# Moving a matmul's two operands apart in SBUF, and alternating the columns of the moving one

## The chip, the cores and the metric

The kernel runs on one core of a Trainium2 chip. The metric is the device time of one execution in microseconds (us). Before the change three runs took 2104.46, 2105.78 and 2109.65 us; the median, 2105.78 us, is what the change is held against.

## The reference

Two layers work on 256 tokens of width 2048, all in fp32. The first mixes by a wide causal convolution and a pooling branch, the second by a short gated convolution; each is followed by a gated feed-forward part of width 5632.

```python
h = x
for i in range(DEPTH):                       # DEPTH = 2
    j = i // 2
    if i % 2 == 0:
        h = h + conv_pool_mixer(h, mix_norm_e[j], w_in_e[j], conv_w_e[j], ...)
    else:
        h = h + short_conv_mixer(h, mix_norm_o[j], w_in_o[j], conv_w_o[j], w_out_o[j])
    h = h + swiglu(rms_norm(h, ffn_norm[i]), w_gate[i], w_up[i], w_down[i])
return rms_norm(h, final_norm)

def swiglu(h, w_gate, w_up, w_down):
    return (jax.nn.silu(h @ w_gate) * (h @ w_up)) @ w_down
```

Everything that is costly in it is a product of 256 tokens with a weight matrix. All weights together are some 5,900 blocks of 128x128.

## The kernel before, in words

Activations lie transposed: features on the 128 partitions, the 256 tokens (`T`) along the free dimension, a tensor of 2048 features as 16 chunks. Each weight block is used once. Blocks stream from HBM in the order of their use (`fetch`, L100, up to 16 blocks of 64 KB to a DMA on SP's queue), and `prepare` (L106) splits eight of them at a time into two float32r tiles: `hi`, a rounded copy made by ScalarE (L114), and `lo`, the rest, made by VectorE (L121, by GpSimd for a range of blocks in the first mixer). Activations are split in the same way by `split` (L193): a chunk of a moving tensor is 512 columns, first the 256 of its high half and then the 256 of its low half, 2048 bytes in each partition.

`product` (L161) multiplies one block with one chunk. In the wide form (all of both feed-forward parts but their last output chunk, and the whole second mixer) it issues two matmuls: `hi` with all 512 columns (L163, the high halves' product lands in the left half of a PSUM bank and the cross term in the right), and `lo` with the 256 high columns, added to the right half (L164). In the narrow form (the first mixer, and the last output chunk) there are three matmuls of 256 columns (L166 to L168). Every matmul comes with a weight load of its own (LDWEIGHTS, PEld in the profile), which reads 128 columns of `hi` or `lo`, 512 bytes in each partition, while the matmul before it streams.

The stages, in order of time: the first mixer (narrow; its moving tensors are `xs`, the normalized input, and `cat`, the mixer's inner result); then the first feed-forward part in two halves, each of 704 wide products on `xs` and 352 on `y` (the gated inner result); the second mixer with 768 wide products on `xs` and 256 on `z`; and the second feed-forward part like the first, with 330 wide and 22 narrow products on the last `y`. The order of the work on each engine comes from a scheduler when the program is built. It is the same, instruction by instruction, before and after the change on all five engines; only operands' addresses and patterns differ.

Where the operands lie matters for what follows. In the built program each `hi` and `lo` tile starts at 64 modulo 256 bytes, and blocks in it are 512 bytes apart, so every weight load starts at 64 modulo 256. `xs` starts at 64, `cat` at 96, `y` and `z` at 160 modulo 256, and their chunks are 2048 bytes apart. Each moving operand therefore stands at one fixed distance past its weights, modulo 256: `xs` at 0, `cat` at 32, `y` and `z` at 96 bytes. (The low half of a chunk starts 1024 bytes behind the high half, which is the same place modulo 256.)

Of the kernel before, what the change touches and what calls it, by code (L numbers as in the profile page):

```python
# [12 lines left out]
F32R = mybir.dt.float32r  # L13
# [4 lines left out]
P = 128  # L18
T = 256
D = 2048  # L20
NC = D // P
DC = 1024
NA = DC // P
FF = 5632
NF = FF // P
NH = NF // 2
# [40 lines left out]
PIECE = 8  # L67
PIECES = [(u, o, min(PIECE, n - o)) for u, n in enumerate(UNITS) for o in range(0, n, PIECE)]

LOOK = 4  # L70
AHEAD = 1

WARM = 9

KEEP = 8

POOL_SPLIT = range(96, 24 * NC + 16 + 7 * NC + 8)

# [6 lines left out]
def block_kernel(ctx: ExitStack, tc: tile.TileContext, xT: bass.AP, xtok: bass.AP, vec: bass.AP, wall: bass.AP, out: bass.AP):  # L85
    nc = tc.nc
    const = ctx.enter_context(tc.tile_pool(name="const", bufs=1))
    act = ctx.enter_context(tc.tile_pool(name="act", bufs=1))
# [8 lines left out]
    cursor = [0, 0]  # L97
    relief = []

    def fetch(u):  # L100
        if u < len(UNITS) and u not in loaded:
            n, off = UNITS[u], UNIT_AT[u] * P * P
            loaded[u] = w = wst.tile([P, 16 * P], F32, name="w")
            nc.sync.dma_start(w[:, : n * P], wall[off : off + n * P * P].rearrange("(p f) -> p f", p=P))  # L104

    def prepare(i):  # L106
        if i >= len(PIECES) or i in ready:
            return
        u, o, n = PIECES[i]
        fetch(u)  # L110
        w = loaded[u][:, o * P : (o + n) * P]
        hi = whl.tile([P, PIECE * P], F32R, name="hi")
        lo = whl.tile([P, PIECE * P], F32R, name="lo")
        nc.scalar.copy(hi[:, : n * P], w)  # L114
        engine = nc.vector
        if UNIT_AT[u] + o in POOL_SPLIT:
            if relief:
                relief.pop()
            else:
                engine = nc.gpsimd  # L120
        engine.tensor_tensor(out=lo[:, : n * P], in0=w, in1=hi[:, : n * P], op=ALU.subtract)  # L121
        ready[i] = (hi, lo)

    def next_block():
        b, i = cursor
        at = UNIT_AT[PIECES[i][0]] + PIECES[i][1]
# [28 lines left out]
    def drain():  # L155
        while any(queues.values()):
            for q in queues.values():
                if q:
                    q.popleft()[1]()

    def product(acc, hi, lo, x, first, last, wide):  # L161
        if wide:
            nc.tensor.matmul(acc, hi, x, start=first, stop=False, skip_group_check=True)  # L163
            nc.tensor.matmul(acc[:, T:], lo, x[:, :T], start=False, stop=last, skip_group_check=True)  # L164
        else:
            nc.tensor.matmul(acc[:, :T], hi, x[:, :T], start=first, stop=False)  # L166
            nc.tensor.matmul(acc[:, :T], hi, x[:, T:], start=False, stop=False)  # L167
            nc.tensor.matmul(acc[:, :T], lo, x[:, :T], start=False, stop=last)  # L168

    def matmul_chunks(xs, ks, n=1, wide=False, behind=None):  # L170


        accs = [ps.tile([P, 2 * T], F32, name="acc") for _ in range(n)]
        for i, k in enumerate(ks):
            first, last = i == 0, i == len(ks) - 1
            for acc in accs:
                hi, lo = next_block()
                product(acc, hi, lo, xs[:, k, :], first, last, wide)
                tick()
            if behind is not None:  # L180
                behind(k)
        return accs
# [22 lines left out]
    def col(name, i):  # L205
        return v[:, VECS[name] + i : VECS[name] + i + 1]

    identity = v[:, VECS["identity"] :]
    h = act.tile([P, NC, T], F32, name="h")
    xs = act.tile([P, NC, 2 * T], F32R, name="xs")  # L210
    ones = const.tile([P, P], F32, name="ones")
    nc.gpsimd.memset(ones, 1.0)

# [14 lines left out]
    def rsqrt_of(*totals, scale, halves=False, st=None):  # L228
# [42 lines left out]
    class Norm:  # L271


        def __init__(self, gain, final=False):
            self.gain, self.final = gain, final
            self.sums = []

        def add(self, c):
# [6 lines left out]

        def scale(self, c):
            if not self.final:
                split(xs[:, c, :], h[:, c, :], col(self.gain, c))

        def square(self, c):  # L290
            if c == 0:
# [37 lines left out]
        return s  # L329


    norm = Norm("mix_norm_e")
    nc.sync.dma_start(v[:, :NC], vec[:, :NC])

    def load(at, n):
# [30 lines left out]
    every = range(NC)  # L366
    with tc.tile_pool(name="m0", bufs=1) as m0, tc.tile_pool(name="ps_side", bufs=2, space=PSUM) as ps_side:
# [1 line left out]
        a_in = m0.tile([P, NA, pad + T], F32, name="a_in")  # L369
        nc.gpsimd.memset(a_in[:, :, :pad], 0.0)  # L370
        conv = m0.tile([P, NA, T], F32, name="conv")
        cat = m0.tile([P, NA, 2 * T], F32R, name="cat")
        total = m0.tile([P, 2, T], F32, name="total")

        sides, prods, state = {}, {}, {}
# [113 lines left out]
        first = matmul_chunks(xs, every, n=4, behind=loads_behind)  # L489
# [42 lines left out]

        project(xs, POOL_CHUNKS)
        drain()
        norm = Norm("ffn_norm0")
        project(cat, range(NA), norm)

    def swiglu(norm, following):
        with tc.tile_pool(name="ffn", bufs=1) as fp:
            phase[0] = fp  # L540
            y = fp.tile([P, NH, 2 * T], F32R, name="y")
            r = None
            for half in range(2):
                for f in range(NH):
                    (acc_g,) = matmul_chunks(xs, every, wide=True)
                    (acc_u,) = matmul_chunks(xs, every, wide=True)
                    if r is None:
                        r = norm.rstd()
                    gate = scaled(acc_g, r, "gate", True)
                    up = scaled(acc_u, r, "val", True)  # L550
                    nc.scalar.activation(gate, gate, AF.Silu)
                    nc.vector.tensor_tensor(out=up, in0=up, in1=gate, op=ALU.mult)
                    split(y[:, f, :], up)
                project(y, range(NH), following if half else None, wide=True, narrow_end=half and following.final)
# [1 line left out]
    x0.close()  # L556


    after = Norm("mix_norm_o")
    swiglu(norm, after)  # L560


    norm = Norm("ffn_norm1")
    with tc.tile_pool(name="m1", bufs=1) as m1:
        phase[0] = m1
        z = m1.tile([P, NC, 2 * T], F32R, name="z")
        pad = SW - 1
        r = None
        for c in range(NC):
            (acc_c,) = matmul_chunks(xs, every, wide=True)  # L570
            (acc_v,) = matmul_chunks(xs, every, wide=True)
# [12 lines left out]
            (acc_b,) = matmul_chunks(xs, every, wide=True)  # L584
# [7 lines left out]
    swiglu(norm, last)  # L592
# [93 lines left out]
```

## Time and profile before

| what | value |
|---|---|
| median of three runs | 2105.78 us |
| the profiled execution, its own time | 2103.73 us |
| its span in the profile | 2102.0 us |
| TensorE (PE) busy | 2079.1 us, 99% |
| weight loads (PEld) busy | 1855.8 us, 88% |
| VectorE (DVE), ScalarE (ACT), GpSimd (POOL) busy | 66%, 50%, 10% |
| HBM traffic | 187 GB/s over the span |

The profiled execution lies 2 us below the median and 1.7 us above its span, so a saving read from the trace can be taken off the median as it stands. Busy time of PE is no measure of how well it works: a matmul's end is modelled, and one is shown as running while the next has begun. What can be trusted are the starts, and so the distance from one start to the next; I call it the pitch.

### The profile page before, as it was taken

The page shows a single profiled execution, that of the slowest core. Times are in us where ns is not written, and L with a number is a line of the kernel's source. Part 1 is how long each engine was busy: PE and PEld are TensorE (multiplying, and loading weights), DVE is VectorE, ACT ScalarE, POOL GpSimd, SP SyncE. Part 2 cuts the span into 40 slices and gives each one's busy share as a digit, 9 for nine tenths or more (in the row PEclk, how much of TensorE's full clock was granted, in tenths as well). Part 3 has the DMA queues.
Part 4 walks back from the last instruction along what each step waited for, and adds up shares of the span by engine and source line. Part 5 has one row for each costly group of instructions (what it writes and reads, how often), then busy time and mean ns, then how long its engine had stood idle before and what let it go on. Part 6 is the DMA issues. An engine that isn't in the chain of part 4 may idle for free.

```text
span 2102.0 us, 31608 instructions
## 1 busy us (share of the span) xinstructions
PE 2079.1 (99%) x12584; PEld 1855.8 (88%) x12584; DVE 1383.4 (66%) x1979; ACT 1060.9 (50%) x1571; POOL 200.6 (10%) x180
## 2 busy tenths in 40 slices
PE   8999999999999999999999999999999999999998
PEld 8999988888888888888888888888888888888887
DVE  6888866666556666666777777666666556666654
ACT  7776654444444444454444445554444444444453
POOL 3985200000000000011000001100000000000011
PEclk9999999999999999999999999999999999999999
DMA  8554455555555555555555555555555555555551
GB/s 326 187 191 168 158 184 197 183 198 182 194 185 188 193 187 194 183 196 182 183 198 182 198 183 193 180 189 198 183 196 184 189 192 183 198 182 199 182 192 68
DMA packets 56884, 395.53 MB, mean 188 GB/s; under 512 B 6432, under 2 KB 7200, under 8 KB 9760
## 3 DMA queue, kind: packets, MB, share of 16 engines
q1 hardware_dynamic: 56736, 393.52, 52.4%
q8 instruction: 98, 1.61, 0.3%
q14 instruction: 50, 0.41, 0.1%
HBM read 391.39 MB, written 2.10 MB: 187 GB/s over the span
## 4 chain that ended last, share of the span: by engine, by line
PE 98%; DMA 1%; DVE 1%; ACT 0%; SPq 0%; issue 0%; DVEq 0%; ACTq 0%
PE acc L163 57%; PE acc L164 30%; PE acc L166 4%; PE acc L168 4%; PE acc L167 4%; DMA rows<-in_xtok 0%; DMA h<-in_xT 0%; DVE res L603 0%; ACT hi L114 0%; PE st L237 0%; PE st L268 0%; DVE lo L121 0%; SPq L104 0%; ACT conv L475 0%; PE idle L243 0%
## 5 line engine op out<-in xcount | busy, mean ns | idle before, releaser
L114 ACT CAST hi<-w 128x1024 fp32r<-128x1024 f32 (+1 forms) x740 | 776.1, 1050 | 975.3 <-PE acc L163 621.0
L121 DVE TENSOR_TENSOR lo<-w,hi 128x1024 fp32r<-128x1024 f32 (+1 forms) x691 | 845.2, 1224 | 639.5 <-ACT hi L114 635.3
L163 PE MATMUL acc<-xs,hi 128*128 128x512 f32 x3584 | 1243.3, 391 | 0.0
L164 PE MATMUL acc<-xs,lo 128*128 128x256 f32 x3584 | 1004.7, 280 | 0.0
L163 PEld LDWEIGHTS acc<-xs,hi 128*128 128x128 f32 x3584 | 670.4, 187 | 146.2
L164 PEld LDWEIGHTS acc<-xs,lo 128*128 128x128 f32 x3584 | 678.1, 189 | 0.1
L163 PE MATMUL acc<-y,hi 128*128 128x512 f32 x1386 | 485.2, 393 | 0.0
L164 PE MATMUL acc<-y,lo 128*128 128x256 f32 x1386 | 386.4, 279 | 0.0
L163 PEld LDWEIGHTS acc<-y,hi 128*128 128x128 f32 x1386 | 259.4, 187 | 61.7
L164 PEld LDWEIGHTS acc<-y,lo 128*128 128x128 f32 x1386 | 259.9, 187 | 0.4
L298 POOL TENSOR_TENSOR sumsq<-sumsq,sq 128x256 f32<-128x256 f32 x56 | 58.8, 1050 | 1599.1 <-ACT sq L296 1599.1
L166 PE MATMUL acc<-xs,hi 128*128 128x256 f32 x512 | 144.0, 284 | 5.2 <-ACT hi L114 4.2
L167 PE MATMUL acc<-xs,hi 128*128 128x256 f32 x512 | 143.6, 283 | 0.0
L168 PE MATMUL acc<-xs,lo 128*128 128x256 f32 x512 | 141.3, 284 | 0.1
L121 POOL TENSOR_TENSOR lo<-w,hi 128x1024 fp32r<-128x1024 f32 x49 | 118.7, 2441 | 43.1 <-PE acc L167 34.3
L166 PEld LDWEIGHTS acc<-xs,hi 128*128 128x128 f32 x512 | 98.1, 192 | 6.2 <-ACT hi L114 5.0
L167 PEld LDWEIGHTS acc<-xs,hi 128*128 128x128 f32 x512 | 98.2, 192 | 0.0
L168 PEld LDWEIGHTS acc<-xs,lo 128*128 128x128 f32 x512 | 96.5, 192 | 0.5 <-DVE lo L121 0.5
L163 PE MATMUL acc<-z,hi 128*128 128x512 f32 x256 | 89.6, 393 | 0.0
L188 ACT COPY cross<-acc 128x256 f32<-128x256 f32 x224 | 80.6, 360 | 0.0
L164 PE MATMUL acc<-z,lo 128*128 128x256 f32 x256 | 71.3, 279 | 0.0
L318 DVE TENSOR_TENSOR h<-acc,h 128x256 f32<-128x256 f32 x112 | 47.2, 423 | 18.9 <-PE acc L168 13.2
(134 smaller groups left out, 1198.6 us busy)
## 6 DMA issues: line engine op xcount, KB each, us to landing
w<-in_wall SPq DMA_DIRECT2D x365, 1024.0 KB, 4.8
w<-in_wall SPq DMA_DIRECT2D x7, 512.0 KB, 7.7
rows<-in_xtok SPq DMA_DIRECT2D x2, 1024.0 KB, 7.9
h<-in_xT SPq DMA_DIRECT2D x7, 256.0 KB, 7.3
out<-res SPq DMA_DIRECT2D x2, 512.0 KB, 2.8
out<-res SPq DMA_DIRECT2D x2, 384.0 KB, 2.8
v<-in_vec SPq DMA_DIRECT2D x1, 260.0 KB, 6.7
h<-in_xT SPq DMA_DIRECT2D x2, 128.0 KB, 2.3
```

Of the source, the lines that this page charges most:

```text
L114: nc.scalar.copy(hi[:, : n * P], w)
L121: engine.tensor_tensor(out=lo[:, : n * P], in0=w, in1=hi[:, : n * P], op=ALU.subtract)
L163: nc.tensor.matmul(acc, hi, x, start=first, stop=False, skip_group_check=True)
L164: nc.tensor.matmul(acc[:, T:], lo, x[:, :T], start=False, stop=last, skip_group_check=True)
L166: nc.tensor.matmul(acc[:, :T], hi, x[:, :T], start=first, stop=False)
L167: nc.tensor.matmul(acc[:, :T], hi, x[:, T:], start=False, stop=False)
L168: nc.tensor.matmul(acc[:, :T], lo, x[:, :T], start=False, stop=last)
L188: nc.scalar.copy(t, acc[:, T:])
L298: nc.gpsimd.tensor_tensor(out=self.sums[0], in0=self.sums[0], in1=sq, op=ALU.add)
L318: nc.vector.tensor_tensor(out=h[:, n, :], in0=acc[:, :T], in1=h[:, n, :], op=ALU.add)
```

## The change

Two things about the moving operand of a matmul change. No instruction is added, removed or moved to another place in any engine's order.

First, where it lies. The moving tensors get tiles with some room at the end, and a helper places them at a chosen byte offset in that room. In the built program `xs` now stands 32 bytes past its weights modulo 256 in the first mixer and 160 past them afterwards, `cat` 32 (as before), and `y` and `z` 160.

Second, in the wide form the order in which the columns of the first matmul (on `hi`) are streamed. Where it was the 256 high columns and then the 256 low ones, it may now be `w` high ones, `w` low ones, the next `w` high ones, and so on. The output is addressed by the same pattern, so every column still lands where it did. `w` depends on the stage: columns in the old order (`w` = 0) in the first half of the first feed-forward part, 32 in its second half, 64 in the second mixer, 8 in the first half of the second feed-forward part and 16 in its second half. The second matmul (on `lo`), and the narrow form, keep their order.

```diff
+_m0, _ffn = 24 * NC + 16 + NC * NC, 3 * NH * NC
+ORDER = {_m0: 0, _m0 + _ffn: 32, _m0 + 2 * _ffn: 64, _m0 + 2 * _ffn + 64 * NC: 8, _m0 + 3 * _ffn + 64 * NC: 16}
...
+XS_M0 = 32
+XS_F0 = 160
+XS_M1 = 160
+XS_F1 = 160
+Y_F0 = 64
+Y_F1 = 64
+Z_M1 = 64
+CAT = 0
...
     def product(acc, hi, lo, x, first, last, wide):
         if wide:
-            nc.tensor.matmul(acc, hi, x, start=first, stop=False, skip_group_check=True)
+            w = ORDER[max(b for b in ORDER if b < cursor[0])]
+            out, x2 = (a.rearrange("p (h b w) -> p b h w", h=2, w=w) if w else a for a in (acc, x))
+            nc.tensor.matmul(out, hi, x2, start=first, stop=False, skip_group_check=True)
             nc.tensor.matmul(acc[:, T:], lo, x[:, :T], start=False, stop=last, skip_group_check=True)
...
-    xs = act.tile([P, NC, 2 * T], F32R, name="xs")
+    xs_room = act.tile([P, NC * 2 * T + 64], F32R, name="xs")
+
+    def moving(room, at, n):
+
+        return room[:, at // 4 : at // 4 + n * 2 * T].rearrange("p (c t) -> p c t", c=n)
...
     class Norm:
-        def __init__(self, gain, final=False):
+        def __init__(self, gain, at=0, final=False):
             self.gain, self.final = gain, final
+            self.xs = moving(xs_room, at, NC)
...
         def scale(self, c):
             if not self.final:
-                split(xs[:, c, :], h[:, c, :], col(self.gain, c))
+                split(self.xs[:, c, :], h[:, c, :], col(self.gain, c))
...
-        cat = m0.tile([P, NA, 2 * T], F32R, name="cat")
+        cat = moving(m0.tile([P, NA * 2 * T + 32], F32R, name="cat"), CAT, NA)
...
-            y = fp.tile([P, NH, 2 * T], F32R, name="y")
+            y = moving(fp.tile([P, NH * 2 * T + 32], F32R, name="y"), at, NH)
...
-        z = m1.tile([P, NC, 2 * T], F32R, name="z")
+        z = moving(m1.tile([P, NC * 2 * T + 32], F32R, name="z"), Z_M1, NC)
```

More of the change, by code (lines that the diff above doesn't have):

```diff
@@ L329, in scaled @@
         return s
-    norm = Norm("mix_norm_e")
+    norm = Norm("mix_norm_e", XS_M0)
+    xs = norm.xs
     nc.sync.dma_start(v[:, :NC], vec[:, :NC])
@@ L534, in block_kernel, with swiglu @@
         drain()
-        norm = Norm("ffn_norm0")
+        norm = Norm("ffn_norm0", XS_F0)
         project(cat, range(NA), norm)
-    def swiglu(norm, following):
+    def swiglu(norm, following, at):
         with tc.tile_pool(name="ffn", bufs=1) as fp:
             phase[0] = fp
-            y = fp.tile([P, NH, 2 * T], F32R, name="y")
+            y = moving(fp.tile([P, NH * 2 * T + 32], F32R, name="y"), at, NH)
             r = None
@@ L544, in swiglu @@
                 for f in range(NH):
-                    (acc_g,) = matmul_chunks(xs, every, wide=True)
-                    (acc_u,) = matmul_chunks(xs, every, wide=True)
+                    (acc_g,) = matmul_chunks(norm.xs, every, wide=True)
+                    (acc_u,) = matmul_chunks(norm.xs, every, wide=True)
                     if r is None:
@@ L556, in block_kernel @@
     x0.close()
-    after = Norm("mix_norm_o")
-    swiglu(norm, after)
-    norm = Norm("ffn_norm1")
+    after = Norm("mix_norm_o", XS_M1)
+    swiglu(norm, after, Y_F0)
+    norm = Norm("ffn_norm1", XS_F1)
     with tc.tile_pool(name="m1", bufs=1) as m1:
         phase[0] = m1
-        z = m1.tile([P, NC, 2 * T], F32R, name="z")
+        z = moving(m1.tile([P, NC * 2 * T + 32], F32R, name="z"), Z_M1, NC)
         pad = SW - 1
@@ L569, in block_kernel @@
         for c in range(NC):
-            (acc_c,) = matmul_chunks(xs, every, wide=True)
-            (acc_v,) = matmul_chunks(xs, every, wide=True)
+            (acc_c,) = matmul_chunks(after.xs, every, wide=True)
+            (acc_v,) = matmul_chunks(after.xs, every, wide=True)
             if r is None:
@@ L583, in block_kernel @@
                 nc.vector.scalar_tensor_tensor(out=co, in0=cv[:, k : k + T], scalar=v[:, wc + k : wc + k + 1], in1=co, op0=ALU.mult, op1=ALU.add)
-            (acc_b,) = matmul_chunks(xs, every, wide=True)
+            (acc_b,) = matmul_chunks(after.xs, every, wide=True)
             bg = scaled(acc_b, r, "pv", True)
@@ L591, in block_kernel @@
     last = Norm("final_norm", final=True)
-    swiglu(norm, last)
+    swiglu(norm, last, Y_F1)
     halves = rsqrt_of(*last.sums, scale=1.0 / D, halves=True)
```

## The prediction

> **What bounds the kernel now.** I read the engines' shares first, then the groups, and then the busy time by stage, with the stages' bounds set where the moving tensor changes.
>
> ```profile
> span 2102.0 us, 31608 instructions
> PE 2079.1 (99%) x12584; PEld 1855.8 (88%) x12584; DVE 1383.4 (66%) x1979; ACT 1060.9 (50%) x1571; POOL 200.6 (10%) x180
> PE 98%; DMA 1%; DVE 1%; ACT 0%; SPq 0%; issue 0%; DVEq 0%; ACTq 0%
> ...
> L163 PE MATMUL acc<-xs,hi 128*128 128x512 f32 x3584 | 1243.3, 391 | 0.0
> L164 PE MATMUL acc<-xs,lo 128*128 128x256 f32 x3584 | 1004.7, 280 | 0.0
> L163 PE MATMUL acc<-y,hi 128*128 128x512 f32 x1386 | 485.2, 393 | 0.0
> L163 PE MATMUL acc<-z,hi 128*128 128x512 f32 x256 | 89.6, 393 | 0.0
> L166 PE MATMUL acc<-xs,hi 128*128 128x256 f32 x512 | 144.0, 284 | 5.2 <-ACT hi L114 4.2
> ```
>
> 98% of the chain that ended last is PE, and the wide matmuls (L163, L164) have no idle time before them. So nothing feeds PE too late; the only question is how long each matmul occupies it. The mean of 391 ns is no answer, since matmuls overlap in these records. The pitch is read from the stages. The rows below are, in this order, the stages on `xs`, `y`, `xs`, `y`, `xs`, `z`, `xs`, `y`, `xs`, `y`; columns are the stretch, its length, each engine's busy time and instructions, the granted clock, and the DMA engines' share and GB/s.
>
> ```profile
> 259.47:504.89 245.42, 245.42 (x1421) 216.60 (x1420) 159.22 (x228) 120.94 (x179) 0.19 (x1) 1.00 0.53 189
> 504.89:628.13 123.24, 123.24 (x706) 107.54 (x705) 67.06 (x78) 51.59 (x61) 0.00 (x0) 1.00 0.52 188
> 628.13:872.19 244.06, 244.06 (x1410) 215.33 (x1409) 157.29 (x218) 117.69 (x175) 0.00 (x0) 1.00 0.54 190
> 872.19:995.43 123.24, 123.24 (x706) 107.54 (x705) 79.72 (x93) 62.40 (x91) 13.93 (x14) 1.00 0.53 188
> 995.43:1263.03 267.60, 267.60 (x1548) 236.15 (x1547) 192.87 (x295) 120.60 (x163) 1.52 (x16) 1.00 0.53 189
> 1263.03:1352.67 89.64, 89.64 (x514) 78.09 (x513) 65.13 (x83) 49.00 (x79) 13.83 (x14) 1.00 0.53 188
> 1352.67:1598.08 245.41, 245.41 (x1420) 216.58 (x1419) 159.54 (x229) 119.80 (x179) 0.19 (x1) 1.00 0.53 189
> 1598.08:1721.33 123.25, 123.25 (x707) 107.41 (x705) 67.14 (x78) 51.62 (x61) 0.00 (x0) 1.00 0.53 188
> 1721.33:1965.39 244.06, 244.06 (x1410) 215.35 (x1409) 157.28 (x218) 117.65 (x175) 0.00 (x0) 1.00 0.54 190
> 1965.39:2080.92 115.53, 115.53 (x662) 100.64 (x661) 60.13 (x71) 57.82 (x83) 17.52 (x13) 1.00 0.42 150
> sum 1821.45, PE 1821.45 PEld 1601.23 DVE 1165.39 ACT 869.12 POOL 47.18; mean PE 182.15 PEld 160.12 DVE 116.54 ACT 86.91 POOL 4.72
> ```
>
> These stages hold 1821.45 of the 2102.0 us, at a full granted clock (1.00), with PE never idle, while DVE is busy 73% at most (65.13 of 89.64) and the DMA engines 54%. One wide product, a pair of matmuls with 512 and 256 columns, takes 244.06 / 704 = 346.7 ns on `xs` and 123.24 / 352 = 350.1 ns on `y`; on `z` it is 89.64 / 256 = 350.2. Same instructions, same columns, same engine loads; `xs` lies 0 and `y` and `z` 96 bytes past the weights modulo 256. That is a first sign that the distance matters, if a small one: 1%.
>
> The narrow form gives a second. The first row is a stretch wholly on `xs` (distance 0), the second wholly on `cat` (distance 32), both of 256-column matmuls; after it four starts in a row on `cat`, and two on `xs`.
>
> ```profile
> 60.00:140.00 80.00, 80.00 (x669) 80.00 (x668) 71.90 (x133) 62.76 (x113) 73.56 (x42) 1.00 0.53 187
> 222.00:258.00 36.00, 36.00 (x311) 36.00 (x310) 33.04 (x43) 24.88 (x43) 11.61 (x13) 1.00 0.51 179
> ```
>
> ```profile
> 239.76 0.28 PE L168 MATMUL acc<-cat,lo 128*128 128x256 f32 x1
> 239.87 0.28 PE L166 MATMUL acc<-cat,hi 128*128 128x256 f32 x1
> 239.99 0.28 PE L167 MATMUL acc<-cat,hi 128*128 128x256 f32 x1
> 240.11 0.28 PE L168 MATMUL acc<-cat,lo 128*128 128x256 f32 x1
> 240.23 0.28 PE L166 MATMUL acc<-cat,hi 128*128 128x256 f32 x1
> ...
> 100.16 0.28 PE L167 MATMUL acc<-xs,hi 128*128 128x256 f32 x1
> 100.28 0.28 PE L168 MATMUL acc<-xs,lo 128*128 128x256 f32 x1
> ```
>
> The counts hold the two or three matmuls that overlap a stretch's edge (0.28 us shown each, at a pitch of 0.12). Without them 80.00 / 666.7 = 120.0 ns on `xs`, 36.00 / 308.7 = 116.6 on `cat`: 3.4 ns, or 2.8%, for 32 bytes of distance. On `cat` the pitch is uneven, one in four about 0.11 us and the others 0.12, so a matmul there can go faster than any on `xs`. DVE and ACT don't make the difference: PE had no idle time in either stretch.
>
> My reading: while a matmul streams its moving columns, the next weight load reads 512 bytes of the same partitions; where both want the same part of memory, the stream stops for a moment, and the distance decides how often.
>
> **The first part: the distance.** In the first mixer `xs` goes from 0 to 32, where `cat` has been all along. 512 narrow products of three matmuls at 3.4 ns make 5.2 us. The idle time of 5.2 us before L166 is no part of the pitch, and DVE's 71.90 of 80.00 us leaves room for 3%. Between nothing (where this stage waits for weights anyway) and 5.2 I take 4.5 us.
>
> For the wide form the distance of 160 is nowhere in this trace. The bounds come from the nearest rows. On the bad side a pair costs what it costs at 96: 350.1 ns, so the 3584 pairs on `xs` lose 3.4 ns each, 12 us, and the 1642 on `y` and `z` stay. On the good side every matmul comes down as far as the fastest one in four on `cat`, an estimate of 113.3 ns (four pitches make 466 at a mean of 116.6; with three of them near 118 some 113 are left), 6.7 ns below `xs`: 13.4 per pair on `xs`, to 333.3, and 16.8 on `y` and `z`: 48 + 28 = 76 us. Between them lies `cat`'s mean: 3.4 ns for a matmul, 6.8 a pair, so 340 ns, from 346.7 and 350.1. I take this one, because it is the only other distance whose effect is measured per weight load, and the load is the same in both forms. 3584 x 6.7 = 24.0 and 1642 x 10.1 = 16.6: **40.6 us**.
>
> The page "TensorE: Matmul & The Clock Gate" of the Trainium skill (Step-by-step: what each phase is for) has it otherwise: the array has two independent read ports, and loading the next weights takes no read bandwidth from the running matmul. By that rule the distance is worth nothing and the 40.6 us are 0. The 120.0 against 116.6 ns here do not agree with it.
>
> **The second part: the order of columns.** It touches only the `hi` matmul, on 1056 pairs with `w` = 32, 1024 with 64, 1056 with 8 and 1034 with 16; 1056 keep the old order. No row of this trace has a matmul with such a pattern. It moves no byte more. What it changes is how fast the moving address advances: two blocks of `w` columns start at the same place modulo 256, so with 8, 16 and 32 the position advances half as fast on average, while with 64 columns (256 bytes) it goes round as before. If the weight load advances more slowly than the stream, which the trace does not resolve, the two might keep their distance and meet less. The best that can be is again 333.3 ns a pair, 6.7 below my 340: on 3146 pairs 21 us more. On the other side a change of half may cost time. There are 512 / `w` of them in a matmul: 16, 8, 64 and 32, or 16,896 + 8,192 + 67,584 + 33,088 = 125,760 in all. One lost column (120.0 / 256 = 0.47 ns) at each makes 59 us. Between a gain of 21 and a loss of 59 I take 0: the pattern stays in whole runs of at least 32 bytes, and the mean of what the patterns can save has no row behind it.
>
> **The sum.** 40.6 + 4.5 + 0 = 45 us. Against the profiled execution's 2103.73 that is 2059, and against the median, 2 us higher, **2061 us**. What is hidden so far stays hidden: at 340 ns a pair DVE rises from 73 to 75% on `z`, and the DMA engines from 54 to 55%. Should PE gain the whole 76 us, DVE is at 76% there, and still nobody waits for it.
>
> **The rivals.**
>
> *The alternation helps too.* The stages with 8, 16 and 32 fall to the best pitch and the others to 340, or all fall further than `cat`'s mean: 2061 - 21 = 2040, at the bound for all 2106 - 76 - 5 = 2025. For it speaks that `cat`'s pitch comes in different values with identical instructions, so that the meeting of the two streams is a matter of their phase. Against it: nothing here shows how fast a weight load advances.
>
> *The change of half costs a column.* The place is L163's successor in the four stages with `w` above 0, the price 0.47 ns for each change. 59 us less the 45 gained leaves 14: 2120 us. From 45 / 125,760 = 0.36 ns a change it decides the sign. It would be plain by stage: +30 ns a pair with 8, +15 with 16, +7.5 with 32, +4 with 64. For it: matmuls with simple rows alone stand in the trace, so nothing vouches for others. Against it: the changes come at whole multiples of 32 bytes.
> The page "PSUM — Partial Sum Buffer" of the Trainium skill (Specifications) gives lines of 8 bytes, and says that any pattern that is not contiguous slows matmuls significantly. The smallest run here is 32 bytes, and no run here shows what that costs.
>
> *The distance means nothing for the wide form.* 346.7 against 350.1 could come from other differences between the tensors, and 160 may do as 0 does. Then only the 4.5 us of the first mixer are left: 2101, or with 96's price 2113. For it: the change from 0 to 96 made only 1%. Against it: `z` and `y` are of different stages and agree to 0.1 ns.
>
> **How the numbers follow.** My forecast, between 2045 and 2085, has a chance of 0.47. The better case, 2015 to 2045, 0.23. No effect on the wide form, 2095 to 2113, 0.13. The costly alternation, above 2105, 0.17. The range should leave out no more than 2 in 10: from 2020, a little below the good bound, to 2115, which takes in the case without effect and the mild part of the costly one. About 0.3%, 6 us, can be told from no change here. Faster than 2099.5: the first two cases, and a little of the third and fourth, 0.73. Within 6 us: 0.10. Slower than 2112: 0.17.
>
> **What would show it.** In the table by stage of the changed kernel: the first stage on `xs` keeps the old order, so its row shows the distance alone, 704 x 340 = 239 us and a little for the norm's matmuls instead of 245.42; its `y` 120 instead of 123.24. If it stays at 245, the distance is worth nothing. The other stages against this one show the alternation, with pitches for 64 as for 0. If 8 is the slowest, 16 next and 32 next, changes of half cost time. The stretch on `xs` in the first mixer should show the 116.6 ns of `cat`. The number of instructions stays. Wrong it would all be if PE showed idle time in the wide stages, for then a weight tile would come too late.

## The result, and the profile after

The changed kernel takes 2127.86 us (median of three runs, 2126.92 to 2128.59) against 2105.78 before: 1.0105 times as long, with a 95% interval of 1.0091 to 1.0119. Forecast was 2061 us and a gain; the measured time lies above the range.

The span grew by 24.1 us, and the engines' shares of it stay within one percent of the old ones. First lines of the changed kernel's profile (L179 and L180 are what L163 and L164 were):

```profile
span 2126.1 us, 31608 instructions
PE 2103.8 (99%) x12584; PEld 1853.1 (87%) x12584; DVE 1383.3 (65%) x1979; ACT 1060.8 (50%) x1571; POOL 200.3 (9%) x180
...
L179 PE MATMUL acc<-xs,hi 128*128 128x512 f32 x3584 | 1265.5, 398 | 0.0
```

In the wide matmuls PE still waits for nothing. The `hi` matmuls have become longer in the records (391 to 398 ns on `xs`), while the `lo` matmuls of L180 stand at 280 ns as before. Which `hi` matmuls they are, the busy time by stage tells, over the same ten stages as before (`xs`, `y`, `xs`, `y`, `xs`, `z`, `xs`, `y`, `xs`, `y`):

```profile
256.20:501.62 245.42, 245.42 (x1421) 216.20 (x1420) 159.13 (x228) 121.06 (x179) 0.18 (x1) 1.00 0.52 189
501.62:623.65 122.03, 122.03 (x706) 107.40 (x705) 67.02 (x78) 51.54 (x61) 0.00 (x0) 1.00 0.53 189
623.65:872.40 248.75, 248.75 (x1411) 214.15 (x1410) 157.23 (x218) 117.64 (x175) 0.00 (x0) 1.00 0.52 187
872.40:996.77 124.37, 124.37 (x707) 107.07 (x705) 79.72 (x93) 62.34 (x91) 13.86 (x14) 1.00 0.51 186
996.77:1264.37 267.60, 267.60 (x1549) 235.73 (x1548) 192.83 (x295) 120.67 (x163) 1.52 (x16) 1.00 0.53 189
1264.37:1353.13 88.76, 88.76 (x515) 78.15 (x514) 65.14 (x83) 48.96 (x79) 13.85 (x14) 1.00 0.52 189
1353.13:1607.89 254.76, 254.76 (x1421) 216.67 (x1420) 159.61 (x229) 119.75 (x179) 0.21 (x1) 1.00 0.51 182
1607.89:1734.62 126.73, 126.73 (x707) 107.62 (x706) 67.12 (x78) 51.45 (x61) 0.00 (x0) 1.00 0.52 183
1734.62:1986.88 252.26, 252.26 (x1411) 216.69 (x1410) 157.25 (x218) 117.53 (x175) 0.00 (x0) 1.00 0.51 184
1986.88:2105.10 118.22, 118.22 (x662) 101.55 (x661) 60.17 (x71) 57.77 (x83) 17.48 (x13) 1.00 0.41 146
...
60.00:140.00 80.00, 80.00 (x688) 1.00 0.55 193
```

Divided by the pairs in it, a stage gives its pitch. Where the columns keep their order, a pair on `y` takes 122.03 / 352 = 346.7 ns (350.1 before), and the first `xs` stage is at its old 245.42 us: the distance of 160 does for the wide form what 0 does, no more. (The first, fifth and seventh stage hold some matmuls of the norm beside their pairs.) Alternation by 64 columns changes nothing (the `xs` stage of the second mixer stays at 267.60 us; `z`, 88.76 / 256, is at 346.7). Alternation by 32 makes it 353.3 (248.75 / 704), by 16 358.3 (252.26 / 704), by 8 360.0 (126.73 / 352). In the first mixer, `xs` goes from 120.0 to 80.00 / 685.7 = 116.7 ns a matmul, as forecast. (The count holds two or three matmuls that overlap the edges, here and below.) The wide stages together grew by 27.4 us, the first mixer gave 3.3 back; that is the 24.1.

### The profile page after: what moved, and what is told of

The parts are those of the page before. It is cut to its first block, busy times and chain, and to the rows that moved or that the text cites. A ratio compares the mean times of both kernels' runs of the same rounds, so it can differ in the third digit from the quotient of the medians.

```text
span 2126.1 us, 31608 instructions
## 1 busy us (share of the span) xinstructions
PE 2103.8 (99%) x12584; PEld 1853.1 (87%) x12584; DVE 1383.3 (65%) x1979; ACT 1060.8 (50%) x1571; POOL 200.3 (9%) x180
## 4 chain that ended last, share of the span: by engine, by line
PE 98%; DMA 1%; DVE 1%; ACT 0%; SPq 0%; issue 0%; DVEq 0%; ACTq 0%
PE acc L179 58%; PE acc L180 29%; PE acc L182 3%; PE acc L184 3%; PE acc L183 3%; DMA rows<-in_xtok 0%; DMA h<-in_xT 0%; DVE res L626 0%; ACT hi L128 0%; PE st L258 0%; PE st L289 0%; DVE lo L135 0%; SPq L118 0%; ACT conv L498 0%; PE idle L264 0%
## 5 line engine op out<-in xcount | busy, mean ns | idle before, releaser
L179 PE MATMUL acc<-xs,hi 128*128 128x512 f32 x3584 | 1265.5, 398 | 0.0
L180 PE MATMUL acc<-xs,lo 128*128 128x256 f32 x3584 | 1003.9, 280 | 0.0
L179 PEld LDWEIGHTS acc<-xs,hi 128*128 128x128 f32 x3584 | 675.5, 188 | 169.0
L180 PEld LDWEIGHTS acc<-xs,lo 128*128 128x128 f32 x3584 | 674.3, 188 | 0.1
L179 PE MATMUL acc<-y,hi 128*128 128x512 f32 x1386 | 491.3, 400 | 0.0
L180 PE MATMUL acc<-y,lo 128*128 128x256 f32 x1386 | 387.5, 280 | 0.0
L179 PEld LDWEIGHTS acc<-y,hi 128*128 128x128 f32 x1386 | 261.2, 189 | 67.3
L180 PEld LDWEIGHTS acc<-y,lo 128*128 128x128 f32 x1386 | 260.9, 188 | 0.4
L179 PE MATMUL acc<-z,hi 128*128 128x512 f32 x256 | 88.7, 392 | 0.0
L180 PE MATMUL acc<-z,lo 128*128 128x256 f32 x256 | 71.4, 280 | 0.0
```

Of the source, the lines that this page charges most:

```text
L179: nc.tensor.matmul(out, hi, x2, start=first, stop=False, skip_group_check=True)
```

## The experiments

All of them are the changed kernel with other distances and other patterns. Distance is again where the moving operand starts past its weights, modulo 256. The stages issue the same products, so one run can hold ten settings, one for each stage, or thirty in thirds. The stages do differ in how a row of matmuls begins, and for some settings that turned out to matter (it is shown with the narrow form below). The edits are shown abridged, with the distances as comments. The theories: (1) the stream of moving columns and the weight load meet in SBUF, and how the moving address walks modulo 256 against the weights' decides the cost; (2) every jump of the moving address costs; (3) the alternating writes to PSUM cost.

### The distances alone

```diff
-ORDER = {_m0: 0, _m0 + _ffn: 32, _m0 + 2 * _ffn: 64, ...: 8, ...: 16}
+PLAN = [(10000, 0, 0)]          # every product: columns in the old order
```

> The change with its distances (32 in the first mixer, 160 for all wide products) and with every product's columns in the old order. If the alternation is what made the changed kernel slower, every wide stage shows the 347 ns a pair that the changed kernel shows where it kept the old order: y and z fall from 350.1 to 347.0 (1642 x 3.1 = 5 us), the first mixer keeps its 3 us, and the time is 2105.8 - 8 = 2098 us (2095 to 2101). If instead the new places slow later stages for another reason (what was measured in the first half of the first feed-forward part does not hold for the others), some of the stages stay at 353 to 362 ns and the time is near 2115 or above.

2094.69 us (five runs, 2093.80 to 2095.04) against 2104.58 of the kernel before on the same chip: 0.9949 of its time, interval 0.9935 to 0.9962; that is just under the range that was expected. Some stretches of its profile by PE's busy time (first mixer on `xs`, then a stage on `y` and one on `xs`):

```profile
60.00:140.00 80.00, 80.00 (x688) 1.00 0.55 195
501.76:623.80 122.04, 122.04 (x706) 1.00 0.53 191
623.80:867.86 244.06, 244.06 (x1411) 1.00 0.52 189
```

Every wide pair is at 346.7 ns. So the two parts of the change come apart: the distances gain some 10 us, and the alternation costs 33 (2127.86 less 2094.69). From the pitches it is 1056 x 6.6 + 1056 x 13.3 + 1034 x 11.6 = 33.0 us for 32, 8 and 16, and nothing for 64.

### Distances in the old order of columns

```diff
-XS_F0 = 160 ...
+XS_M0, XS_F0, XS_M1, XS_F1 = (64, 32, 64, 128)      # and y 192, 224, 32, 128; z 64; cat 128
```

> Columns in the old order everywhere; the distance differs by stage: first mixer xs 64, cat 128; wide stages in order xs 32, y 192, xs 32, y 224, xs 64, z 64, xs 128, y 32, xs 128, y 128. If weight load and stream get into each other's way according to their distance, the pitch of the narrow form (120.0 ns at 0, 116.6 at 32) and of the wide pair (346.7 at 0, 350.1 at 96, 347 at 160) takes further values, with at least one wide pair at 343 ns or less. If the distance hardly matters to the wide form, all wide pairs stay within 346 to 351.

A single run takes 2115.25 us. Three of its wide stretches: `xs` at 32 (704 pairs), `y` at 192 (352), `xs` at 128 (704).

```profile
628.48:872.54 244.06, 244.06 (x1410) 1.00 0.53 190
504.13:628.48 124.35, 124.35 (x707) 1.00 0.52 187
1729.39:1976.57 247.18, 247.18 (x1410) 1.00 0.52 187
```

At 32, where the narrow form had been faster on `cat`, the wide pair takes 346.7 ns, exactly what it takes at 0. At 192 it is 353.3, at 128 351.1, at 224 353.3. At 64 it is 349.3 on `z` and 353.3 on the `xs` of the second mixer: one distance, two pitches. In the first mixer a narrow matmul takes about 118 ns at 64 and 119 at 128. So the distance does matter to the wide form, up to 7 ns, but the `xs` of the kernel before already stood at the best value found, and no pair fell to the 343 ns that the first theory had asked for.

### The weights moved instead

```diff
-        hi = whl.tile([P, PIECE * P], F32R, name="hi")
+        hi = whl.tile([P, PIECE * P + 64], F32R, name="hi")[:, 16:]      # the same for lo
```

> Columns in the old order; hi and lo tiles start 64 bytes further, at 128 modulo 256. The first mixer's xs and cat stand where they stood before the change (64 and 96 modulo 256), so their distances are now 192 and 224; wide stages have the distances, in order, xs 192, y 32, xs 192, y 64, xs 224, z 96, xs 32, y 128, xs 32, y 160. If the distance between the operands decides, the first mixer's xs falls from 360.0 to 340.8 ns for three matmuls (what cat at 192 showed) without having been moved, and the wide pairs show what the scan showed: 192 and 224 at 353, 32 and 160 at 346.7, 64 at 349 to 353, 96 at 350, 128 at 351. If the place of the moving operand by itself decides, the first mixer's xs stays at 360 and cat at 350.

A single run takes 2110.85 us. First mixer on `xs`, at the very address it had before the change; then two wide stages on `xs`, at 192 and 32:

```profile
60.00:140.00 80.00, 80.00 (x708) 1.00 0.55 197
626.80:875.53 248.73, 248.73 (x1410) 1.00 0.53 186
1729.75:1973.81 244.06, 244.06 (x1411) 1.00 0.53 190
```

80.00 / 705.7 = 113.4 ns where it was 120.0: with the moving operand left where it was and the weights moved by 64 bytes, the same matmul is 5% faster. The wide pairs follow too: 353.3 at 192, 346.7 at 32. So it is the distance that counts, not the place of either, though it doesn't settle everything: later in this run the same `xs` at the same 192 takes 117.8 ns (its row stands with the narrow form below). The page "TensorE: Matmul & The Clock Gate" of the Trainium skill (Step-by-step: what each phase is for) says that loading the next weights doesn't take read bandwidth from the running matmul. By that, moving the weights alone should change nothing; here it changed the pitch by 6.6 ns.

### Alternation at other distances

```diff
+PLAN: in each stage a third of the products by 32, a third by 16, a third by 8
+distances: xs 0, 64, 128 (and 128 in the first mixer); y 32, 96, 192, 224; z 160; cat 192
```

> Alternation by 32, 16 and 8 columns in thirds of each wide stage, at distances xs 0, y 32, xs 0, y 96, xs 64, z 160, xs 128, y 192, xs 128, y 224; first mixer xs 128, cat 192. Theory 1 (the alternating address advances half as fast modulo 256 and so meets the weight load for longer): the cost over the old order, at distance 160 some 6, 11 and 13 ns a pair for 32, 16 and 8, changes strongly with the distance, by more than 5 ns, and may turn into a gain somewhere. Theory 2 (each change of half costs time by itself): the cost is the same at every distance, within 2 ns.

A single run takes 2160.00 us. Alternation by 32 on `xs` at 0 (240 pairs), on `y` at 32 (110), on `xs` at 128 (240), on `y` at 192 (110):

```profile
637.02:723.40 86.38, 86.38 (x483) 1.00 0.52 184
511.50:550.37 38.87, 38.87 (x222) 1.00 0.52 182
1765.11:1851.48 86.37, 86.37 (x482) 1.00 0.50 182
1638.98:1677.62 38.64, 38.64 (x222) 1.00 0.49 182
```

| distance | old order | by 32 | by 16 | by 8 |
|---|---|---|---|---|
| 0 | 346.7 | 359.9 | 360.0 | 360.0 |
| 32 | 346.7 | 353.4 | 357.8 | 358.3 |
| 96 | 350.1 | 356.0 | 360.0 | 360.0 |
| 128 | 351.1 | 359.9 | 360.0 | 362.2 |
| 160 | 346.7 | 353.4 | 358.3 | 360.0 |
| 192 | 353.3 | 351.3 | 360.0 | 363.3 |
| 224 | 353.3 | 355.0 | 360.0 | 360.0 |

(ns a pair, a stretch's length over its pairs; the column of the old order from the runs above and the kernel before.) The place 64 is left out, since part of its stretches holds the norm's matmuls. By 32 the cost over the old order goes from 13 ns at 0 (the cell is of the second `xs` stage; the first settled at 353.3, a cost of 7) to a gain of 2 at 192. By 16 and 8 the pitch itself is nearly the same everywhere (357.8 to 363.3), so the cost over the old order still goes from 13 ns at 0 to 7 at 224. Theory 2 had asked for the same cost at every distance, within 2 ns; that failed. No cell is under 346.7.

### Reading or writing

```diff
-            out, x2 = (a.rearrange("p (h b w) -> p b h w", h=2, w=w) if w else a for a in (acc, x))
+            out, x2 = paired(acc, write), paired(x, read)     # thirds of a stage: read alone, write alone, both
```

> Distance 160 for all wide products; thirds of each stage alternate the moving columns alone, the output columns alone, and both, by 32 (first xs and y), 16 (second xs and y), 64 (xs and z), 8 (next xs and y) and 4 (last xs and y). Where one side alone alternates, the products land in permuted columns, so the output is not the reference's; no work is left out. Theory 1 (meeting of stream and weight load in SBUF): reading alone costs what both cost, 6, 11, 0 and 13 ns a pair over 347, and writing alone costs nothing. Theory 3 (the alternating writes to PSUM cost): writing alone costs that, reading alone nothing. Theory 2 (a change of half costs in the operand's address generation) could show on either side, growing with the number of changes: at 4 columns, 128 of them, more than at 8.

A single run takes 2130.62 us. By 32 on `y`: reading alone, writing alone, both (110, 132, 110 pairs); then by 16 on `xs` (240, 224, 240); then writing alone by 4 on `y` (132):

```profile
505.39:544.26 38.87, 38.87 (x222) 1.00 0.52 184
544.26:590.03 45.77, 45.77 (x267) 1.00 0.55 196
590.03:628.89 38.86, 38.86 (x222) 1.00 0.50 182
628.89:715.29 86.40, 86.40 (x482) 1.00 0.51 184
715.29:792.95 77.66, 77.66 (x451) 1.00 0.52 190
792.95:879.35 86.40, 86.40 (x483) 1.00 0.51 183
...
2030.12:2075.90 45.78, 45.78 (x267) 1.00 0.54 193
```

Reading alone costs what both cost: 353.4 by 32, 360.0 by 16. By 4, with twice as many changes of half as by 8, it is 363.3 on `xs`, again for either; on `y` both stood at 363, while reading alone began at 363 and went over to 373 in mid-stage. Writing alone stands at 346.7 in every stage, and at 346.8 by 4 columns. Theory 3 has fallen. The page "PSUM — Partial Sum Buffer" of the Trainium skill (Specifications) warns of any pattern that is not contiguous; down to runs of 16 bytes this run shows nothing of it.

### Which reads

```diff
+            return bass.AP(tensor=x.tensor, offset=x.offset, ap=[x.ap[0]] + [list(s) for s in steps])
+# every column twice: ((1, 256), (0, 2));  runs of 32 twice: ((32, 8), (0, 2), (1, 32))
+# jumps between runs of 32, unbroken modulo 256: ((64, 8), (96, 2), (1, 32));  every second column: ((1, 2), (2, 256))
```

> Only the reading of the hi products' columns differs by stretch; output columns in the old order, so columns are wrong and the output is not the reference's, but as many columns are streamed. Distance 160 on xs (first 704, second 704 and 768 pairs) and 0 on y and z. Patterns, each for a quarter of a stage (the last chunk of every sum plain): first stages: every column twice in a row; each run of 32 columns read twice; runs of 32 with a jump of 64 columns between them, so that the address goes on without a break modulo 256; the change's alternation by 32. Second stages: runs of 8 twice, runs of 16 twice, the jump with runs of 16, alternation by 16. Second mixer: every second column, every fourth column, runs of 64 alternating between places 128 bytes apart modulo 256, the jump with runs of 8. Theory 1 (what costs is that the address advances half as fast modulo 256): every column twice, which has no jump at all, costs as much as alternation by 8 (360 ns a pair), runs read twice cost what alternation by the same width costs (353 for 32, 358 to 360 for 16, 360 for 8), and the jumps that keep the walk unbroken cost nothing (347). Theory 2 (each jump of the address costs): every column twice stays at 347, and the jumps cost 353 and more, the shorter the runs the more.

A single run takes 2223.93 us. Stretches on `xs` at 160 of 175 pairs each: runs of 32 read twice, jumps between runs of 32, alternation by 32; runs of 16 twice, jumps between runs of 16; jumps between runs of 8 (191 pairs); last, runs of 64 in turn from two places 128 bytes apart modulo 256 (191 pairs). One pair in 16 in each, the last of its sum, reads plainly:

```profile
311.47:373.32 61.85, 61.85 (x353) 1.00 0.53 187
373.67:434.33 60.66, 60.66 (x352) 1.00 0.52 188
434.68:496.51 61.83, 61.83 (x353) 1.00 0.52 186
...
683.61:746.45 62.84, 62.84 (x352) 1.00 0.51 182
746.80:807.47 60.67, 60.67 (x353) 1.00 0.54 187
1282.20:1348.42 66.22, 66.22 (x384) 1.00 0.52 188
1214.01:1281.85 67.84, 67.84 (x384) 1.00 0.51 178
```

Runs of 32 read twice, without ever going to the low half, cost 353.4 ns, as alternation does (353.3); runs of 16 twice 359.1, as alternation by 16 (359.2). What the two have in common is the walk modulo 256. Jumps of 256 bytes every 32, 16 or 8 columns, chosen so that the walk has no break, cost nothing at distance 160: 60.67 / 175 = 346.7 and 66.22 / 191 = 346.7, the last with some 60 jumps in a matmul. On `y` and `z` at distance 0 they cost 6.6 ns (353.3), the same for 16 jumps and for 64. So theory 2, a price for each jump, has fallen; but theory 1 had asked for no cost at all with an unbroken walk, and at 0 that failed. The runs of 64 cost 8.5 ns (67.84 / 191 = 355.2): each of them walks through all 256 bytes, and only seven times in a matmul does the walk fall out of step, by half a turn.

One pattern went as neither theory said. Starts in the stretch that reads every column twice:

```profile
299.41 0.38 PE L191 MATMUL acc<-xs,hi 128*128 128x512 f32 x1
299.62 0.28 PE L192 MATMUL acc<-xs,lo 128*128 128x256 f32 x1
...
300.41 0.39 PE L191 MATMUL acc<-xs,hi 128*128 128x512 f32 x1
300.64 0.28 PE L192 MATMUL acc<-xs,lo 128*128 128x256 f32 x1
```

The first pair here reads every column twice; the one at 300.41 is the last chunk of its sum, which reads plainly. From `hi` to `lo` it is 0.21 us for the one (215.8 ns in the mean of 163) and 0.23 for the other. Theory 1 asked for a slow walk to cost 360 ns a pair, and this one takes 334. So a slow walk by itself isn't what costs. The alternations and the runs read twice share that they fetch as much as the old order while staying in the same 256 bytes for longer; the runs of 64 and the jumps at distance 0 cost something without that. The cheap pattern asks for half as many different addresses. That a column given twice is fetched once is my reading, not shown. The page "TensorE: Matmul & The Clock Gate" of the Trainium skill (Back-to-back issue gap) gives N / 2.4 + 2.5 ns, 215.8 for 512 columns, for a matmul by itself. An estimate from it: of the 229 ns from `hi` to `lo` in the plain order at 160, some 13 are extra.

### A better place for the narrow form

In the alternation run `cat` stood at 192 and took 340 ns for a product of three matmuls, under the wide pair's 346.7 for as many columns. Three runs followed this up: `xs` and `cat` at 192; the `lo` tiles alone moved by 128 bytes; and all products in the narrow form.

```diff
-XS_M0 = 32
+XS_M0 = 192      # and cat at 192
```

> Like the run with the distances alone, but xs and cat of the first mixer at 192 in place of 32. If the narrow form's 340.8 ns at 192 holds for xs as it did for cat, the first mixer's 656 products save 9.2 ns each, 6 us, where PE is what that stage waits for: 2094.7 - 6 = 2089 us (2087 to 2092). If VectorE and GpSimd hold this stage back (72 and 74 us busy of 80 before), the gain shrinks to 2 us or none.

```diff
-        lo = whl.tile([P, PIECE * P], F32R, name="lo")
+        lo = whl.tile([P, PIECE * P + 64], F32R, name="lo")[:, 32:]
```

> Columns in the old order; lo tiles alone start 128 bytes further, so the two weight loads of a pair have distances that differ by 128: hi / lo in the wide stages in order 160/32, 64/192, 160/32, 96/224, 0/128, 128/0, 32/160, 192/64, 32/160, 224/96. If each matmul is slowed by the weight load that is read while it streams, according to that load's distance alone, the hi matmul's pitch follows the lo tile's distance and the lo matmul's pitch that of hi: with both at a good distance (160/32, 32/160) the pair is at 346.7, with one bad (0/128, 128/0) between 347 and 351. If the two meet as a sequence whose phase carries over, other values appear, and a pair below 346.7 is possible.

The first took 2092.04 us (five runs, 2091.43 to 2092.32), 0.9930 of the kernel before (interval 0.9917 to 0.9944) where 32 had given 0.9949: 3 to 4 us, half of what was expected (in the two traces the first mixer is 2.5 us shorter); the second 2101.41 in a single run. A stretch of the first mixer on `xs` with 192; then, from the run with `lo` moved, the same place with 192 for `hi` and 64 for `lo`, and a wide stage on `xs` at 160/32:

```profile
60.00:100.00 40.00, 40.00 (x342) 1.00 0.55 202
```

```profile
60.00:140.00 80.00, 80.00 (x708) 1.00 0.54 196
620.43:866.83 246.40, 246.40 (x1411) 1.00 0.53 188
```

40.00 / 339.6 = 117.8 ns here, and 113.4 with 192 in the run with the weights moved: the same distance, the same instructions, two pitches. Each of the two runs shows both. After the row of matmuls has been broken near 150 us (by other matmuls and by idle time of PE), the next row on `xs`, still at 192, runs at the other one; first the run with `xs` and `cat` at 192, then that with the weights moved:

```profile
160.00:190.00 30.00, 30.00 (x267) 1.00 0.59 211
```

```profile
160.00:190.00 30.00, 30.00 (x257) 1.00 0.57 210
```

Without the two or three at the edges that is 30.00 / 264.6 = 113.4 and 30.00 / 254.6 = 117.8 ns. In both runs one pitch holds steadily from 60 us up to the break, and the other after it. So at this distance two steady pitches exist, and how a row starts seems to choose between them. That fits a gain of half of what was expected: the longest stretch on `xs` got the poor one.

With `hi` at 192 and `lo` at 64 it is 113.4 again, and there the rows before and after the break agree. The wide pair, where both single distances are good (160/32), has risen to 350.0 instead of staying at 346.7. With the two exchanged (32/160) it stays at 346.7, and so it does at 64/192, where neither single distance was good. So it isn't each load by itself that counts, but the sequence.

```diff
-                    (acc_g,) = matmul_chunks(norm.xs, every, wide=True)
+                    (acc_g,) = matmul_chunks(norm.xs, every)        # and everywhere else; no cross term to copy and add
```

> Every product in the narrow form (three matmuls of 256 columns, all added in one half of a PSUM bank), so the wide form's copy and sum of the cross term are gone, but not a column less is streamed. lo tiles 128 bytes further than hi tiles; distances hi/lo: first mixer 192/64, then the stages in order 192/64, 64/192, 192/64, 224/96, 64/192, 0/128, 160/32, 32/160, 160/32, 192/64. If the weight load that is read during a matmul costs it according to its distance, and 192/64 and 64/192 are good (340.4 and 340.9 ns for three in the run with the lo tiles moved), those stages show 340 to 341 ns a product against the wide form's 346.7: were all stages like that, 5226 x 6.3 = 33 us less than the run with the distances alone, 2062 us. If what made the short stretches of the first mixer fast (its chunks, its gaps) is needed, the long narrow stages show 350 to 360.

> The same with the lo tiles 64 bytes further than hi tiles; distances hi/lo: first mixer 192/128, then 192/128, 0/192, 192/128, 32/224, 128/64, 64/0, 96/32, 160/96, 96/32, 224/160. If both loads' distances add their own cost, a product costs two loads at the hi tile's and one at the lo tile's: with 192 good (113.6 ns) and 128 poor (118.7), 192/128 gives 346, 0/192 gives 354, and no stage is under 340. If instead the sequence's phase decides, values scatter without such an order.

2106.38 and 2142.53 us, a single run each. Narrow stages on `xs` of 704 products: at 192/64 and at 160/32 in the first, at 192/128 and at 96/32 in the second:

```profile
616.54:855.91 239.37, 239.37 (x2115) 1.00 0.54 193
1722.99:1971.75 248.76, 248.76 (x2114) 1.00 0.52 187
```

```profile
635.44:885.12 249.68, 249.68 (x2114) 1.00 0.52 186
1749.81:2003.24 253.43, 253.43 (x2115) 1.00 0.51 183
```

340.0 ns a product at 192/64, in both `xs` stages and on `y`; 353.4 at 160/32, 354.7 at 192/128, 360.0 at 96/32. The expectation that 64/192 would do as well failed (356.7 on `y`), and so did the sum of single costs (0/192: 354 forecast and 353.3 found, but 192/128: 346 against 354.7).

```diff
+XS_M0, XS_F0, XS_M1, XS_F1 = (192, 192, 192, 192)      # y, z and cat at 192 too; lo tiles at 64
```

> Every product narrow, hi tiles at distance 192 and lo tiles at 64 in all stages. Five stretches with these distances showed 340.0 ns a product without exception, so all ten wide stages become 5226 x 340.0 = 1777 us where the run with the distances alone has 5226 x 346.6 = 1811, and the first mixer's 656 products save some 10 ns each, 6 us: 2094.7 - 34 - 6 = 2055 us (2052 to 2060). If the scatter of the other distances comes back in some stages (a start in another phase), those show 353 to 357 ns and the time is up to 2100.

> As that, but the distance of the hi tiles differs by stage in smaller steps (lo 128 less modulo 256): 192 in the first mixer, then in the stages in order 176, 200, 176, 48, 208, 240, 184, 112, 184, 144. If the memory's parts are 32 bytes or wider, 200 and 208 show the 340 ns of 192, and 176 and 184 lie between 160's 353 and that; if 16 bytes or less matter, each value has its own pitch. No pitch under 340 has been seen in the narrow form; one would show that the 32-byte steps missed the best place.

The first takes 2053.90 us (five runs, 2052.42 to 2054.37) where the kernel before took 2105.04: 0.9755 of its time, interval 0.9742 to 0.9769, and within the 2052 to 2060 us that were expected. It beats both kernels. Two stretches of it with all engines (first mixer, a stage on `xs`):

```profile
60.00:140.00 80.00, 80.00 (x709) 80.00 (x708) 76.95 (x142) 66.24 (x120) 76.77 (x43) 1.00 0.55 196
610.87:850.23 239.36, 239.36 (x2114) 239.36 (x2113) 142.43 (x174) 106.43 (x131) 0.00 (x0) 1.00 0.55 194
```

The second is 239.36 / 704 = 340.0 ns a product, and all ten stages have that pitch, though there are three weight loads in it instead of two. The finer steps (2135.22 us in a single run) found nothing better: 16 bytes less (176/48) make it 353.3 in two stages, 8 bytes less (184/56) 353.3 in one stage and 360.0 in another, 8 bytes more (200/72) 360.0, and 208/80 356.7. So the good place is narrow, as far as one or two stages for each value can show it.

## Why the prediction was wrong

**What bounds the kernel** was read rightly: PE without a gap, and the pitch as the only thing to change. In every wide stretch shown here PE is busy from end to end.

**The reading that stream and weight load meet, by their distance,** held in part. That the distance counts is shown: with the weights moved and `xs` left alone, 120.0 ns became 113.4 or 117.8. But one distance can have two pitches, and no run here streams without weight loads, so that the two stop each other is still a reading.

**The distance in the first mixer**, 4.5 us forecast: 3.3 measured. The 116.6 ns of `cat` carried over to `xs` (116.7), the same form at the same distance, and the stretches on `xs` became 4.9 us shorter. Of that, 1.4 us were lost again in the second stretch on `cat`, which keeps its distance: it starts after idle time of PE at a low granted clock (0.51 before, 0.53 after), and that lasted 13 matmuls before and 27 after.

**The distance in the wide form** is one of the two steps that failed. The prediction carried the 3.4 ns of `cat` over "because it is the only other distance whose effect is measured per weight load, and the load is the same in both forms". At `cat`'s own distance of 32 a wide pair takes 346.7 ns, as at 0; at 160 too. Of the 40.6 us forecast the `xs` part, 24.0, was nothing, and the 16.6 on `y` and `z` were 1642 x 3.4 = 5.6 in the run with the distances alone. The trace of before had one distance that both forms share, 96, in the last 22 narrow products, on `y`:

```profile
2080.93:2088.73 7.80, 7.80 (x67) 1.00 0.00 0
```

From its first start to the start of its last matmul, 7.80 us for 65 pitches, that is 120.0 ns a matmul, what `xs` takes at 0; the wide pair was 3.4 ns dearer at 96 than at 0. On that row the transfer from one form to the other already fails; the prediction passed it over.

**The order of columns** is the other step that failed. It was taken at 0 between a gain of 21 us and a loss of 59, and it lost 33 us. This decided the sign. The bound held, the choice inside it did not. The runs on reading and writing and on read patterns showed that the loss comes with reading the moving columns in that order.

**The rival that named the loss** (a column's time at every change of half) had the order of the stages right and the mechanism wrong. It gave 30, 15, 7.5 and 4 ns for 8, 16, 32 and 64; measured are 13.3, 11.6, 6.6 and 0. Jumps that keep the walk modulo 256 unbroken are free at 160, and reading the same run twice, with no change of half, costs what alternation costs. The rival's time, 2120 us, was the nearest of all, because a price too high (59 us against 33) stood against a gain too high (45 against some 10): luck, not mechanism.

**The better case**, in which a slower walk meets the load less, fell with the alternation run: only by 32 at 192 was there a gain, of 2 ns, and from a bad 353.3. That the half-speed walk "might keep its distance" and so meet the load less is not what came: at 160 the alternations and the runs read twice, which stay longer in the same 256 bytes, cost more, and only reading every column twice cost less.

What stays open: why 192/64 locks all narrow stages at 340.0 ns, why the wide pair never came under 346.7 in plain order, and why one distance can show two pitches (192 and 184/56 in the narrow form, 64 in the wide one, alternation by 32 at 0, and alternation by 16 at 160: 358.3 ns in the changed kernel, 360.0 in the run on reading and writing). That the start of a row chooses the pitch fits the narrow form at 192; what in the start does it was not tested, and reading by 4 on `y` changed its pitch without a break. What there is, is a table of settings and no rule that gives it.

## What to carry to other kernels

Where TensorE runs without a gap, measure the pitch from start to start by stage, and compare it between stages whose operands stand at different distances in SBUF: a few per cent may lie in the addresses alone. Such an effect belongs to a whole sequence of loads and streams; do not carry it from one form of product to another, but let one run with a different setting in each stage show it, and look at each setting in more than one row of matmuls, since a row can keep the pitch that it started with. And try the form that looks dearer again at the new addresses: three narrow matmuls held their 340 ns in every row, under the wide pair's 346.7, only with both weight tiles in the right place.

## What the hardware showed beside that

A stream that takes every second column, though in order and with nothing skipped for good, needs nearly twice the time; so does one that takes every fourth. Stretches from the run on read patterns, every second column, then every fourth (191 pairs):

```profile
1020.00:1105.00 85.00, 85.00 (x305) 1.00 0.32 117
...
1105.50:1213.66 108.16, 108.16 (x384) 1.00 0.33 117
```

That is 566 ns a pair for every fourth (108.16 / 191) and 562 for every second (85.00 / 151.3), one plain pair in 16 included, where the plain order takes 346.7. From the start of `hi` to that of `lo` it is 443 and 431 ns in the median, against 229. The page "SBUF — State Buffer" of the Trainium skill (Specifications) asks for two hits in each 16-byte line for full speed. Every second fp32 column has two, every fourth one; the two cost nearly the same, so here a second hit in the line did not help. That what counts is whether columns are neighbours is my reading.
